# Opening of a hybrid decoder layer on one core: weight splits one piece ahead, squares of x in the order in which x lands, memory keys evacuated later, and another bank for a unit

## The chip, the cores and the metric

The kernel runs on one core of one Trainium2 chip. The metric is the device time of one execution in microseconds, the median of several runs. All times below are microseconds.

## What is computed

One decoder layer for 512 tokens of width 1024, in float32, with 256 memory tokens. Cut to what matters here:

```
h = rms_norm(x, g_mix)
proj = h @ w_in                       # queries, keys, values of two branches, q_c, three gates
mkv = rms_norm(mem, g_mem) @ w_mem_kv
mk, mv = split(mkv)                   # 512 columns of keys, 512 of values, 4 heads of 128
mk = rms_norm(heads(mk), g_k_mem);  q_c = rms_norm(heads(q_c), g_q_mem)
y_c = softmax(q_c mk^T / sqrt(128)) mv
merged = sigmoid(a_m) * (y_m @ w_br_moba) + sigmoid(a_f) * (y_f @ w_br_fox) + sigmoid(a_c) * (y_c @ w_br_mem)
x = x + merged @ w_out
x = x + (silu(h2 @ w_gate) * (h2 @ w_up)) @ w_down,   h2 = rms_norm(x, g_ffn)
```

y_m is block-sparse causal attention and y_f attention with a forgetting gate; neither is touched.

## The kernel before

**Products in three passes.** Each float32 operand is split into a high part, rounded to the fast float32 format of TensorE, and a low part, the rest. A product is hi·hi + hi·lo + lo·hi, three matmuls into one PSUM bank (PASSES). So each weight must be split before it is used.

**Pieces.** The weights come as a list of pieces, up to 512 KB each, laid out in the order of their use. `load_next` starts a piece's load on the queue of SP, into a tile `w_raw`. `split_next` issues ScalarE's copy to `w_hi` (L223) and puts VectorE's subtraction to `w_lo` (L226) off to the next call. `take` hands out the next piece; if it is not split yet, it is split then. Pieces 0 to 3 and 4 to 7 are the halves of `w_mem_kv` (keys and values of the memory), 8 to 11 the queries Q_C, and gates and units follow.

**The order of the work is fixed by the code, by ticks.** The engines run what they are given in program order. `mm` issues a matmul and, after every six matmuls of 512 columns, a `tick`. A tick splits one piece if fewer than `pace["ahead"]` pieces stand split beyond those taken, runs what `later(n, fn)` put off for n ticks, and then one step of the side list that `beside` filled. With `pace["ahead"] = 4`, set ahead of the keys, up to four pieces beyond the taken ones are split, and a split stands ahead of the tick's other steps.

**The opening.** `turn_mem` transposes the memory tokens and scales them into `mhT`. `mem_groups` (L497 to 513) makes two PSUM groups (two blocks of 128 memory tokens) over four pieces, first for the keys and then for the values: 48 matmuls of 512 columns each time. It takes both banks from the pool "m" (3 banks, `ps_m`); the pool "a" has 5 (`ps_a`). `head_chunk` (L515) evacuates the keys' groups at once (ScalarE's copy to `raw`, L523), squares them (`sqh`, L525) and sums the squares (VectorE, L526), and `head_rest` normalises them later. The values are evacuated to `memv` (ScalarE L318, VectorE L321). Beside these matmuls runs the side list: `square_x` (L622, ScalarE's sum of squares of one tile of 128 tokens of x), `rms_x` with `scale_x` (L627, tiles 0 and 1 on GpSimd, 2 and 3 on VectorE), `mem_square` (L455), `rms_mem`, and `turn_x` (L639), which transposes two of eight column blocks of x per step through a bank of "a" and evacuates them into `hT` (ScalarE's high part L318, VectorE's low part L321). When the values are done, the side list is flushed and `head_chunk` starts Q_C: its first group of 128 tokens takes the pieces 8 to 11, and `whole_h` (L652) adds up `xf` from `hT` on VectorE, one per tick.

**Units.** `tok_unit` makes 512 tokens by 512 columns from seven products M1 to M7 in the order M1, M2, M5, M6, M3, M7, M4, each in a bank of "m", but M5 in one of "a"; `after` adds each into its sums on VectorE one tick later (`add`, L745). It is called three times. What follows the second unit is `branch_part`, whose groups take banks of "m" and are evacuated by VectorE (L1047).

Of the kernel before, what the change touches and what calls it, by code (L numbers as in the profile page):

```python
# [13 lines left out]
AF = mybir.ActivationFunctionType  # L14
# [8 lines left out]
D = 1024  # L23
# [19 lines left out]
def hybrid_layer(ctx, tc, rope, x, mem, g_mix, w_in, b_forget, g_q_moba, g_k_moba, g_q_fox,  # L43
# [3 lines left out]
    act, dve, pool, pe = nc.scalar, nc.vector, nc.gpsimd, nc.tensor  # L47
# [8 lines left out]
    def slot(name, dt=F32):  # L56
        return U.tile([P, SLOT], dt, name=name, tag="u", bufs=NSLOT)
# [20 lines left out]
    def bank(tag):  # L78
        return psum.tile([P, 512], F32, name="ps_" + tag, tag=tag, bufs=BANKS[tag])

    def sm(name, w, bufs=6):
        return small.tile([P, w], F32, name=name, tag=name, bufs=bufs)
# [75 lines left out]
    raws, split, used = {}, {}, {}  # L158
# [82 lines left out]
    def take(n):  # L241
        while st["split"] < st["take"] + n:
            split_next(n)
        while w_lows:
            w_lows.popleft()()
        run_pend()
        got = [split.pop(st["take"] + j) for j in range(n)]
        st["take"] += n
        return got
# [6 lines left out]
    pace = {"credit": 0.0, "ns": 0, "ahead": 2}  # L256
    QUANTUM = 1250

    pend = []

    def run_pend():
        for fn in pend:
            fn()
        pend.clear()
# [42 lines left out]
    def later(n, fn):  # L307
        deferred.append([n, fn])
# [68 lines left out]
    def load_x():  # L377
        r = slot("x_t")
        t = len(x_t)
        nc.sync.dma_start(r[:, :D], x[0, t * P:(t + 1) * P, :])  # L380
        x_t.append(r)
# [11 lines left out]
    NG = 22  # L393
    GMIX, GFFN, GQF, GQM, GQC, GKF, GKM, GKC = 0, 8, 16, 17, 18, 19, 20, 21
    grow = consts.tile([NG, P], F32, name="grow")
    load_x()
    load_next()
    for _ in range(2):
        load_x()
    nc.gpsimd.dma_start(grow[0:8], g_mix.rearrange("o (k p) -> (o k) p", p=P))  # L400
    nc.gpsimd.dma_start(grow[8:16], g_ffn.rearrange("o (k p) -> (o k) p", p=P))
# [50 lines left out]
    ssp, ssm = sm("ssp", 4, 1), sm("ssm", 2, 1)  # L452
# [22 lines left out]

    def piece_of(W, k):
        for i in range(KD):
            if i == len(W):
                W.extend(take(1))
            n = W[i][0].shape[1]  # L480
            if k < n:
                return W[i], k
            k -= n

    def tok_group(lhs, t, W, n, tag="m"):


        ps = bank(tag)
        nk = len(lhs)
        for k in range(nk):  # L490
            w, j = piece_of(W, k)
            for a, b in PASSES:
                mm(ps[:, :n], lhs[k][a][:, t * P:(t + 1) * P], w[b][:, j, :n], n,
                   (k == 0 and (a, b) == PASSES[0]), (k == nk - 1 and (a, b) == PASSES[-1]))
        return ps

    def mem_groups(amid=None):  # L497


        ps = [bank("m"), bank("m")]  # L500
        for j in range(4):
            W = take(1)[0]
            todo = [(t, k, a, b) for t in range(MT) for k in (2 * j, 2 * j + 1) for a, b in PASSES]
            if amid and j == 0:
                todo.sort(key=lambda x: x[3])
            for n, (t, k, a, b) in enumerate(todo):
                if amid and j == 0 and n == 4:
                    amid()
                mm(ps[t], mhT[k][a][:, t * P:(t + 1) * P], W[b][:, k % 2, :], 512,
                   (k == 0 and (a, b) == PASSES[0]), (k == KD - 1 and (a, b) == PASSES[-1]))  # L510
        return ps

    def head_chunk(ntok, d, blocks, lag=9, pre=None, rows=None):


        W = []
        nh = 512 // d
        raws = [slot("raw") for _ in range(ntok // 2)]
        ss = sm("ss", 32, 4)
        for t in range(ntok):  # L520
            ps = tok_group(hT, t, W, 512) if pre is None else pre[t]
            r = raws[t // 2][:, t % 2 * 512:(t % 2 + 1) * 512]
            act.activation(r, ps, AF.Copy)  # L523
            sq = half_slot("sqh")
            act.activation(sq, r, AF.Square)  # L525
            pend.append(lambda t=t, sq=sq: dve.tensor_reduce(  # L526
                ss[:, t * nh:(t + 1) * nh], sq.rearrange("p (h d) -> p h d", h=nh),
                axis=AX.X, op=OP.add))
        head_rest(raws, 512, ss, ntok, d, "plain", blocks, lag, rows=rows)

    def head_rest(raws, tw, ss, ntok, d, kind, blocks, lag, rows=None, e=2):
# [85 lines left out]
    hT = []  # L617
# [3 lines left out]
    def square_x(t):  # L621
        act.activation(slot("junk")[:, :D], x_t[t][:, :D], AF.Square, accum_out=ssx[:, t:t + 1])  # L622
# [85 lines left out]
    def tok_unit(done):  # L708


        banks, raw = {}, {}
        z = half_slot("zs")

        def after(m):
            if m == "M1":
                act.activation(z, banks.pop(m), AF.Copy)
            elif m == "M2":
                raw[0] = slot("raw")
                add(raw[0][:, 0:512], banks.pop(m), z)
            elif m == "M6":  # L720
                add(z, banks.pop(m), z)
                add(raw[0][:, 512:1024], banks["M5"], z)
            elif m == "M3":
                add(raw[0][:, 512:1024], banks.pop(m), raw[0][:, 512:1024])
                done[0](raw[0])
            elif m == "M7":
                add(z, banks.pop(m), z)
                raw[1] = slot("raw")
                add(raw[1][:, 512:1024], banks.pop("M5"), z)
            elif m == "M4":  # L730
                add(raw[1][:, 0:512], banks.pop(m), z)
                done[1](raw[1])

        for m in ORDER:
            W = take(1)[0]
            ps = banks[m] = bank("a" if m == "M5" else "m")
            for t2 in range(2):
                for k in range(4):
                    for a, b in PASSES:
                        mm(ps[:, t2 * 256:(t2 + 1) * 256], right_of(RIGHT[m], k, a, t2), W[b][:, k, :],  # L740
                           256, (k == 0 and (a, b) == PASSES[0]), (k == 3 and (a, b) == PASSES[-1]))
            later(1, lambda m=m: after(m))
# [36 lines left out]
    rs_mem = sm("rsm", MT, 1)  # L779

    def rms_mem():
        dve.tensor_reduce(ssm, ssp.rearrange("p (t a) -> p t a", a=2), axis=AX.X, op=OP.add)
        rsqrt(ssm, 1.0 / D, 2, 1, out=rs_mem)

    def both(f, *args):
        return lambda: [f(*a) for a in args]

    def last_square(t):
        square_x(t)
        rms_x(t // 2)  # L790

    beside([idle, idle, small_gains, lambda: square_x(0), lambda: last_square(1),
            both(mem_square, (0, 0), (1, 0)), both(mem_square, (0, 1), (1, 1)),
            lambda: square_x(2), lambda: last_square(3), rms_mem, idle]
           + [both(turn_x, (k,), (k + 1,)) for k in range(0, KD, 2)], 1.0)

    turn_mem(0, (split_next, split_next))
    pace["ahead"] = 4
    pre = mem_groups(lambda: turn_mem(1))
    head_chunk(MT, 128, [(GKC, KC, h, gcol) for h in range(4)], lag=22, pre=pre, rows=rs_mem)  # L800
    vslots = [slot("memv", F32R) for _ in range(MT)]
    pre = mem_groups()
    for t in range(MT):
        evac_split(vslots[t][:, 0:512], vslots[t][:, 512:1024], pre[t], rs_mem[:, t:t + 1])
    pre = None
# [383 lines left out]
    B, L, H, banks, got, Z = {}, {}, {}, {}, {}, {}  # L1189
# [61 lines left out]
    for t in range(NT):  # L1251
        r = slot("x1")
# [392 lines left out]
    for n, x in enumerate(order):  # L1645
# [3 lines left out]
        _, m, p = x  # L1649
# [49 lines left out]
```

## Time and profile before

| what | us |
|---|---|
| median of 3 runs | 868.25 (867.46 to 868.31) |
| the profiled execution's own time | 868.44 |
| its span in the profile | 866.6 |
| TensorE's matmuls busy (PE) | 845.9, 98% |
| VectorE (DVE) | 659.1, 76% |
| ScalarE (ACT) | 471.9, 54% |
| GpSimd (POOL) | 226.2, 26% |

The page is one profiled execution. Busy time is the union of an engine's instructions; matmuls are pipelined, so that one row of several shows their common length, and one matmul alone shows its whole length. A number in square brackets behind a timeline row is the idle time of that engine just ahead of it and what ended it. The granted clock of TensorE is given as a share of full speed: 1.00 is 2.4 GHz and 0.50 is 1.2 GHz.

### The profile page before, as it was taken

How to read it: one execution, taken by the hardware profiler on the slowest of the kernel's cores; microseconds unless marked ns; L12 is line 12 of the kernel's file. 1: busy time of each engine (PE TensorE's matmuls, PEld its weight loads, DVE VectorE, ACT ScalarE, POOL GpSimd, SP SyncE). 2: the span in 40 equal slices, each digit the busy share in tenths (PEclk: the TensorE clock that was granted, in tenths of full speed). 3: DMA queues.
4: the chain of work that ended last, by engine and by line, in shares of the span. 5: the costliest groups of instructions: out<-in, count | busy, mean ns of one | idle time of the engine just before them, and what ended most of it. 6: DMA issues, size and time to landing. Idle time of an engine off the chain costs nothing.

```text
span 866.6 us, 13979 instructions
## 1 busy us (share of the span) xinstructions
PE 845.9 (98%) x5204; PEld 756.8 (87%) x5204; DVE 659.1 (76%) x1126; ACT 471.9 (54%) x816; POOL 226.2 (26%) x310
## 2 busy tenths in 40 slices
PE   7799999999999999999999999999999999999998
PEld 5588899799888888988888888999999999988886
DVE  5687599869678477667655936899889898997985
ACT  6755576567766546656534535454333444464671
POOL 5112228221522443434220003233210222110210
PEclk9899999999999999999999999999999999999999
DMA  9923248216430551441692535989885889774992
GB/s 311 339 34 88 59 115 213 39 50 193 114 86 11 162 142 29 135 106 52 179 211 97 171 97 122 216 182 191 169 173 92 177 164 205 178 188 147 232 257 94
DMA packets 141284, 126.10 MB, mean 146 GB/s; under 512 B 5841, under 2 KB 120073, under 8 KB 141217
## 3 DMA queue, kind: packets, MB, share of 16 engines
q1 hardware_dynamic: 107840, 95.21, 37.2%
q0 software_dynamic: 32192, 27.89, 21.0%
q10 hardware_dynamic: 1184, 2.12, 0.8%
q8 instruction: 41, 0.67, 0.3%
q14 instruction: 27, 0.21, 0.1%
HBM read 116.79 MB, written 4.21 MB: 140 GB/s over the span
## 4 chain that ended last, share of the span: by engine, by line
PE 80%; DVE 10%; ACT 5%; DMA 2%; issue 1%; POOL 1%; SPq 0%; DVEq 0%; ACTq 0%; POOLq 0%
PE ps_m L291 38%; PE ps_a L1369 12%; PE ps_m L1369 9%; PE ps_a L1522 9%; PE ps_a L959 3%; PE ps_m L1522 3%; DMA w_raw<-in_w_mem_kv_dram 2%; DVE w_lo L226 2%; PE ps_a L897 2%; PE ps_a L948 2%; ACT w_hi L223 1%; DVE wl L1230 1%; DVE w_sum L212 1%; DVE qT L587 1%; DVE xl L1315 1%
## 5 line engine op out<-in xcount | busy, mean ns | idle before, releaser
L226 DVE TENSOR_TENSOR w_lo<-w_raw,w_hi 128x1024 fp32r<-128x1024 f32 (+2 forms) x88 | 108.4, 1243 | 33.9 <-ACT w_hi L223 33.2
L291 PE MATMUL ps_m<-w_hi,hT 128*128 128x256 f32 (+2 forms) x464 | 122.0, 337 | 0.0
L291 PE MATMUL ps_m<-hT,w_hi 128*128 128x512 f32 x384 | 121.0, 396 | 0.0
L1369 PE MATMUL ps_a<-xh,wl 128*128 128x256 f32 x352 | 100.0, 284 | 1.0 <-DVE wl L1230 0.8
L1369 PE MATMUL ps_a<-xh,wh 128*128 128x256 f32 x352 | 99.8, 283 | 0.2 <-ACT wh L1227 0.2
L1369 PE MATMUL ps_a<-xl,wh 128*128 128x256 f32 x352 | 99.6, 283 | 0.0
L223 ACT ACTIVATE w_hi<-w_raw 128x1024 fp32r<-128x1024 f32 (+2 forms) x88 | 86.3, 1002 | 4.1 <-issue 2.5
L291 PEld LDWEIGHTS ps_m<-w_hi,hT 128*128 128x128 f32 x464 | 80.1, 189 | 7.1
L291 PEld LDWEIGHTS ps_m<-hT,w_hi 128*128 128x128 f32 x384 | 69.7, 189 | 12.8
L1522 PE MATMUL ps_a<-dh,dr 128*128 128x512 f32 x242 | 76.6, 390 | 0.1
L291 PE MATMUL ps_m<-w_lo,hT 128*128 128x256 f32 (+2 forms) x232 | 75.9, 327 | 0.0
L291 PE MATMUL ps_m<-hT,w_lo 128*128 128x512 f32 x192 | 75.0, 391 | 0.0
L1369 PE MATMUL ps_m<-xl,wh 128*128 128x256 f32 x264 | 74.7, 283 | 0.0
L1369 PE MATMUL ps_m<-xh,wh 128*128 128x256 f32 x264 | 74.7, 283 | 0.0
L1369 PE MATMUL ps_m<-xh,wl 128*128 128x256 f32 x264 | 74.7, 283 | 0.0
L1412 ACT ACTIVATE z<-z 128x512 f32<-128x512 f32 x22 | 13.9, 633 | 105.3 <-DVE z L745 105.3
L1204 POOL DMA_DIRECT2D wq<-in_w_gate_dram x22 | 30.6, 1389 | 153.2 <-DMA wq<-in_w_gate_dram 49.0
L1369 PEld LDWEIGHTS ps_a<-xh,wl 128*128 128x128 f32 x352 | 67.5, 192 | 1.6 <-DVE wl L1230 1.6
L1230 DVE TENSOR_TENSOR wl<-wq,wh 128x1024 fp32r<-128x1024 f32 x55 | 66.9, 1218 | 2.1 <-ACT wh L1227 1.6
L1369 PEld LDWEIGHTS ps_a<-xh,wh 128*128 128x128 f32 x352 | 67.5, 192 | 0.4 <-ACT wh L1227 0.4
L1369 PEld LDWEIGHTS ps_a<-xl,wh 128*128 128x128 f32 x352 | 67.6, 192 | 0.0
L930 POOL TENSOR_SCALAR p_t<-p_t,rc 128x128 f32<-128x128 f32 (+1 forms) x64 | 39.2, 613 | 108.1 <-DVE rc L929 92.9
(271 smaller groups left out, 2211.1 us busy)
## 6 DMA issues: line engine op xcount, KB each, us to landing
w_raw<-in_w_in_dram SPq DMA_DIRECT2D x45, 512.0 KB, 4.3
wq<-in_w_gate_dram SPq DMA_DIRECT2D x55, 256.0 KB, 5.2
wq<-in_w_up_dram SPq DMA_DIRECT2D x55, 256.0 KB, 5.7
dq<-in_w_down_dram SPq DMA_DIRECT2D x25, 512.0 KB, 5.9
wq<-in_w_gate_dram POOLq DMA_DIRECT2D x22, 256.0 KB, 7.9
wq<-in_w_up_dram POOLq DMA_DIRECT2D x22, 256.0 KB, 10.2
dq<-in_w_down_dram POOLq DMA_DIRECT2D x10, 512.0 KB, 8.2
w_raw<-in_w_mem_kv_dram SPq DMA_DIRECT2D x8, 512.0 KB, 8.9
```

The lines of the kernel that those rows point to most:

```text
L223: act.activation(hi[:, c], r[:, c], AF.Copy)
L226: dve.tensor_tensor(lo[:, c], r[:, c], f32(hi[:, c]), op=OP.subtract)
L291: pe.matmul(ps, lhsT, rhs, start=start, stop=stop)
L897: pe.matmul(ps[:, :n], Q[p][:, s * 512 + i * P:s * 512 + (i + 1) * P], K[p][s][:, b * 512:b * 512 + n], start=b == 0, stop=b == 1)
L930: pool.tensor_scalar(pt[:, :nk], pt[:, :nk], rc, 1.0, op0=OP.mult, op1=OP.mult)
L948: pe.transpose(tb[:, j * P:(j + 1) * P], pt[:, j * P:(j + 1) * P], ident)
L959: pe.matmul(yb[:, :256], V[p][:, j, 2 * s:2 * s + 2, :], PT[b][:, j, :], start=(j == 0 and b == 0), stop=(j == nj - 1 and b == 1))
L1204: e.dma_start(t[:, g * 512:(g + 1) * 512].rearrange("p (k c) -> p k c", k=4), dsrc(w, kh * 512 * DFF + f0 + fh * P, [[DFF, P], [P * DFF, 4 ...
L1230: dve.tensor_tensor(full(lo), full(r), f32(full(hi)), op=OP.subtract)
L1369: pe.matmul(ps[:, g * 256:(g + 1) * 256], w[a][:, g, k, :], r[b][:, k, :], start=n % 12 == 0, stop=n % 12 == 11)
L1412: act.activation(z[:, :, 0, :], z[:, :, 0, :], AF.Silu, scale=1.0 - 2 * j)
L1522: pe.matmul(acc_d[m][t2], r[a][:, e * 256 + t2 * P:e * 256 + (t2 + 1) * P], w[b][:, e * 512:(e + 1) * 512], start=(p == 0 and e == 0 and ( ...
```

## The change

Six edits, all on the order of things; every product and sum remains.

1. The loads: the fifth weight piece is loaded ahead of the second tile of x and not behind it.
2. `pace["ahead"]` stays 2 in the keys, becomes 1 with their last piece, and 4 with the last piece of the values (then 2, as before).
3. The side list squares the tiles 2 and 3 of x in one step, ahead of the second pair of memory squares; `rms_mem` runs after 12 ticks instead of in the list.
4. The evacuation of the keys is put off by 3 and 4 ticks, their squares by 5 and 6.
5. The second bank of the values comes from "a".
6. M4 of the units takes its bank from "a".

```diff
@@ -393,9 +393,8 @@
     NG = 22
     GMIX, GFFN, GQF, GQM, GQC, GKF, GKM, GKC = 0, 8, 16, 17, 18, 19, 20, 21
     grow = consts.tile([NG, P], F32, name="grow")
-    load_x()
     load_next()
-    for _ in range(2):
+    for _ in range(3):
         load_x()
     nc.gpsimd.dma_start(grow[0:8], g_mix.rearrange("o (k p) -> (o k) p", p=P))
     nc.gpsimd.dma_start(grow[8:16], g_ffn.rearrange("o (k p) -> (o k) p", p=P))
@@ -497,9 +496,11 @@
     def mem_groups(amid=None):
 
 
-        ps = [bank("m"), bank("m")]
+        ps = [bank("m"), bank("m" if amid else "a")]
         for j in range(4):
             W = take(1)[0]
+            if j == 3:
+                pace["ahead"] = 1 if amid else 4
             todo = [(t, k, a, b) for t in range(MT) for k in (2 * j, 2 * j + 1) for a, b in PASSES]
             if amid and j == 0:
                 todo.sort(key=lambda x: x[3])
@@ -517,15 +518,21 @@
         nh = 512 // d
         raws = [slot("raw") for _ in range(ntok // 2)]
         ss = sm("ss", 32, 4)
-        for t in range(ntok):
-            ps = tok_group(hT, t, W, 512) if pre is None else pre[t]
-            r = raws[t // 2][:, t % 2 * 512:(t % 2 + 1) * 512]
-            act.activation(r, ps, AF.Copy)
+        def square(t, r):
             sq = half_slot("sqh")
             act.activation(sq, r, AF.Square)
-            pend.append(lambda t=t, sq=sq: dve.tensor_reduce(
+            pend.append(lambda: dve.tensor_reduce(
                 ss[:, t * nh:(t + 1) * nh], sq.rearrange("p (h d) -> p h d", h=nh),
                 axis=AX.X, op=OP.add))
+
+        for t in range(ntok):
+            r = raws[t // 2][:, t % 2 * 512:(t % 2 + 1) * 512]
+            if pre is None:
+                act.activation(r, tok_group(hT, t, W, 512), AF.Copy)
+                square(t, r)
+            else:
+                later(3 + t, lambda r=r, ps=pre[t]: act.activation(r, ps, AF.Copy))
+                later(5 + t, lambda t=t, r=r: square(t, r))
         head_rest(raws, 512, ss, ntok, d, "plain", blocks, lag, rows=rows)
 
     def head_rest(raws, tw, ss, ntok, d, kind, blocks, lag, rows=None, e=2):
@@ -733,7 +740,7 @@
 
         for m in ORDER:
             W = take(1)[0]
-            ps = banks[m] = bank("a" if m == "M5" else "m")
+            ps = banks[m] = bank("a" if m in ("M5", "M4") else "m")
             for t2 in range(2):
                 for k in range(4):
                     for a, b in PASSES:
@@ -780,7 +787,7 @@
 
     def rms_mem():
         dve.tensor_reduce(ssm, ssp.rearrange("p (t a) -> p t a", a=2), axis=AX.X, op=OP.add)
-        rsqrt(ssm, 1.0 / D, 2, 1, out=rs_mem)
+        rsqrt(ssm, 1.0 / D, 2, 0, out=rs_mem)
 
     def both(f, *args):
         return lambda: [f(*a) for a in args]
@@ -790,12 +797,12 @@
         rms_x(t // 2)
 
     beside([idle, idle, small_gains, lambda: square_x(0), lambda: last_square(1),
-            both(mem_square, (0, 0), (1, 0)), both(mem_square, (0, 1), (1, 1)),
-            lambda: square_x(2), lambda: last_square(3), rms_mem, idle]
+            both(mem_square, (0, 0), (1, 0)), lambda: [square_x(2), last_square(3)], idle,
+            both(mem_square, (0, 1), (1, 1)), idle]
            + [both(turn_x, (k,), (k + 1,)) for k in range(0, KD, 2)], 1.0)
+    later(12, rms_mem)
 
     turn_mem(0, (split_next, split_next))
-    pace["ahead"] = 4
     pre = mem_groups(lambda: turn_mem(1))
     head_chunk(MT, 128, [(GKC, KC, h, gcol) for h in range(4)], lag=22, pre=pre, rows=rs_mem)
     vslots = [slot("memv", F32R) for _ in range(MT)]
```

On the queue of SP the first tiles of x (`x_t`) and the weight pieces (`w_raw`) stood so before:

```order
L380 DMA x_t_86<-in_x_dram 128x1024
L380 DMA x_t_94<-in_x_dram 128x1024
L179 DMA w_raw_96<-in_w_mem_kv_dram 128x2x512
L380 DMA x_t_98<-in_x_dram 128x1024
L380 DMA x_t_100<-in_x_dram 128x1024
```

and stand so now:

```order
L380 DMA x_t_86<-in_x_dram 128x1024
L179 DMA w_raw_94<-in_w_mem_kv_dram 128x2x512
L380 DMA x_t_96<-in_x_dram 128x1024
L380 DMA x_t_98<-in_x_dram 128x1024
L380 DMA x_t_100<-in_x_dram 128x1024
```

The piece has passed the second tile of x. ScalarE, from the split of the piece 5 on (`w_hi_284`, then 6, 7, 8), with the squares of the memory (`sqm`), the keys' evacuation and squares (`raw`, `sqh`) and the squares of x (`junk`), before:

```order
L223 ACTIVATE w_hi_284<-w_raw_200 128x1024
L455 ACTIVATE sqm_294,ssp_130<-mem_h_78 128x512 x2
L523 ACTIVATE raw_303<-ps_m_160 128x512
L525 ACTIVATE sqh_306<-raw_303 128x512
L523 ACTIVATE raw_303<-ps_m_161 128x512
L525 ACTIVATE sqh_306<-raw_303 128x512
L223 ACTIVATE w_hi_321<-w_raw_214 128x1024
L622 ACTIVATE junk_326,ssx_132<-x_t_98 128x1024
L223 ACTIVATE w_hi_335<-w_raw_252 128x1024
L622 ACTIVATE junk_340,ssx_132<-x_t_100 128x1024
L223 ACTIVATE w_hi_354<-w_raw_270 128x1024
```

and now, where the pieces 5, 6, 7 are `w_hi_314`, `w_hi_342` and `w_hi_378`:

```order
L629 ACTIVATE junk_289,ssx_132<-x_t_98 128x1024
L629 ACTIVATE junk_291,ssx_132<-x_t_100 128x1024
L223 ACTIVATE w_hi_314<-w_raw_200 128x1024
L347 ACTIVATE ra_295<-rv_293 128x2
L348 ACTIVATE ry_294<-ra_295 128x2
L454 ACTIVATE sqm_333,ssp_130<-mem_h_78 128x512 x2
L223 ACTIVATE w_hi_342<-w_raw_214 128x1024
L534 ACTIVATE raw_304<-ps_m_160 128x512
L534 ACTIVATE raw_304<-ps_m_161 128x512
L318 ACTIVATE hT_361<-ps_a_356,gcol_123 128x512
L318 ACTIVATE hT_369<-ps_a_364,gcol_123 128x512
```

The squares of x stand ahead of piece 5 and no longer behind 6 and 7; the keys' copies stand behind piece 6, their squares later still, and the first two evacuations of x ahead of piece 7.

VectorE around the start of Q_C, from the third low part of `hT` on; the pieces 8 to 10 had been split ahead of this, and `w_lo_450` is 11:

```order
L321 SCALAR_TENSOR_TENSOR hT_432<-ps_a_427,gcol_123,hT_432 128x512
L321 SCALAR_TENSOR_TENSOR hT_440<-ps_a_435,gcol_123,hT_440 128x512
L321 SCALAR_TENSOR_TENSOR hT_461<-ps_a_456,gcol_123,hT_461 128x512
L321 SCALAR_TENSOR_TENSOR hT_469<-ps_a_464,gcol_123,hT_469 128x512
L226 TENSOR_TENSOR w_lo_450<-w_raw_338,w_hi_449 128x1024
L321 SCALAR_TENSOR_TENSOR hT_484<-ps_a_479,gcol_123,hT_484 128x512
L321 SCALAR_TENSOR_TENSOR hT_492<-ps_a_487,gcol_123,hT_492 128x512
L321 SCALAR_TENSOR_TENSOR memv_314<-ps_m_316,rsm_133,memv_314 128x512
L321 SCALAR_TENSOR_TENSOR memv_315<-ps_m_317,rsm_133,memv_315 128x512
L652 TENSOR_TENSOR xf_509<-hT_406 128x512
L652 TENSOR_TENSOR xf_509<-hT_414 128x512
L652 TENSOR_TENSOR xf_529<-hT_432 128x512
```

and now from the seventh, where `w_lo_442`, `w_lo_473`, `w_lo_493` and `w_lo_510` are the pieces 8 to 11:

```order
L321 SCALAR_TENSOR_TENSOR hT_454<-ps_a_449,gcol_123,hT_454 128x512
L321 SCALAR_TENSOR_TENSOR hT_462<-ps_a_457,gcol_123,hT_462 128x512
L226 TENSOR_TENSOR w_lo_442<-w_raw_270,w_hi_441 128x1024
L321 SCALAR_TENSOR_TENSOR memv_310<-ps_m_312,rsm_133,memv_310 128x512
L321 SCALAR_TENSOR_TENSOR memv_311<-ps_a_313,rsm_133,memv_311 128x512
L226 TENSOR_TENSOR w_lo_473<-w_raw_317,w_hi_472 128x1024
L659 TENSOR_TENSOR xf_500<-hT_361 128x512
L226 TENSOR_TENSOR w_lo_493<-w_raw_345,w_hi_492 128x1024
L659 TENSOR_TENSOR xf_500<-hT_369 128x512
L226 TENSOR_TENSOR w_lo_510<-w_raw_381,w_hi_509 128x1024
```

The low parts of Q_C's four pieces stand now between the last evacuations and `xf`, one after the other. In the units, the sum of M4 reads `ps_a` instead of `ps_m`.

## Rows read from the trace of the kernel before

**Rows 1.** The page: the span, and the busy time of each engine (its share of the span, its instructions).

```profile
span 866.6 us, 13979 instructions
PE 845.9 (98%) x5204; PEld 756.8 (87%) x5204; DVE 659.1 (76%) x1126; ACT 471.9 (54%) x816; POOL 226.2 (26%) x310
```

**Rows 2.** The waits of TensorE, by what ended them: us in total, times, the longest.

```profile
PE ps_a L639 <- DVE x_t L627: 5.1, 2, 4.9
PE ps_m L291 <- DVE raw L745: 1.4, 1, 1.4
PE ps_m L291 <- ACT raw L523: 1.1, 1, 1.1
```

**Rows 3.** The chain of work that ended last, in order of time, from 36 to 62 us: start, length, engine and operation, count.

```profile
36.96 2.56 PE ps_m L291 x6
...
40.84 1.40 PE ps_m L291 x6
42.24 0.87 PE ps_a L639 x8
...
45.37 16.35 PE ps_m L291 x72
```

**Rows 4.** Windows: the stretch and its length, then the busy time (instructions) of PE, PEld, DVE, ACT and POOL, the granted clock of TensorE, the DMA share, GB/s.

```profile
33.50:40.30 6.80, 5.15 (x17) 4.17 (x18) 6.20 (x14) 2.59 (x5) 1.37 (x1) 0.50 1.08 340
...
22.73:52.03 29.30, 23.03 (x105) 18.62 (x104) 22.37 (x35) 21.15 (x35) 3.76 (x3) 0.88 0.92 261
...
60.00:70.00 10.00, 10.00 (x49) 8.18 (x48) 7.18 (x12) 5.50 (x9) 0.00 (x0) 1.00 0.00 0
...
80.00:90.00 10.00, 10.00 (x54) 8.45 (x53) 4.64 (x6) 5.05 (x7) 3.45 (x4) 1.00 0.73 159
```

**Rows 5.** The timeline of ScalarE in the opening: start, length, line, operation, tiles.

```profile
17.33 1.06 ACT L622 ACTIVATE junk<-x_t 128x1024 f32<-128x1024 f32 x1 [0.27 <-DMA x_t<-in_x_dram]
...
18.64 1.06 ACT L223 ACTIVATE w_hi<-w_raw 128x1024 fp32r<-128x1024 f32 x1 [0.16 <-DMA w_raw<-in_w_mem_kv_dram]
19.60 0.19 ACT L347 ACTIVATE ra<-rv 128x2 f32<-128x2 f32 x1
...
19.93 0.62 ACT L455 ACTIVATE sqm<-mem_h 128x512 f32<-128x512 f32 x1
...
22.58 1.06 ACT L223 ACTIVATE w_hi<-w_raw 128x1024 fp32r<-128x1024 f32 x1 [1.32 <-DMA w_raw<-in_w_mem_kv_dram]
...
24.77 0.57 ACT L523 ACTIVATE raw<-ps_m 128x512 f32<-128x512 f32 x1
25.37 0.63 ACT L525 ACTIVATE sqh<-raw 128x512 f32<-128x512 f32 x1
...
28.01 1.05 ACT L622 ACTIVATE junk<-x_t 128x1024 f32<-128x1024 f32 x1
...
42.72 1.27 ACT L318 ACTIVATE hT<-ps_a,gcol 128x512 fp32r<-128x512 f32 x2
...
52.23 0.60 ACT L523 ACTIVATE raw<-ps_m 128x512 f32<-128x512 f32 x1 [2.86 <-PE ps_m L291]
```

**Rows 6.** The timeline of TensorE's matmuls: the values' first matmul in its second bank, and the last matmul of Q_C's first group (the first of the two).

```profile
25.39 0.50 PE L291 MATMUL ps_m<-w_hi,mhT 128*128 128x512 f32 x1 [1.15 <-ACT raw L523]
...
51.81 0.62 PE L291 MATMUL ps_m<-w_hi,hT 128*128 128x512 f32 x2
```

**Rows 7.** The timeline of VectorE in the opening.

```profile
26.04 0.69 DVE L526 TENSOR_REDUCE ss<-sqh 128x4 f32<-128x512 f32 x1 [1.14 <-ACT sqh L525]
...
32.44 1.22 DVE L226 TENSOR_TENSOR w_lo<-w_raw,w_hi 128x1024 fp32r<-128x1024 f32 x1
33.58 0.16 DVE L351 TENSOR_TENSOR ra<-ry 128x2 f32<-128x2 f32 x1
...
34.16 1.42 DVE L627 TENSOR_SCALAR x_t<-x_t,rr 128x1024 f32<-128x1024 f32 x2
...
47.22 1.40 DVE L321 SCALAR_TENSOR_TENSOR memv<-ps_m,rsm,memv 128x512 fp32r<-128x512 f32 x2
48.53 1.88 DVE L652 TENSOR_TENSOR xf<-hT 128x512 f32<-128x512 f32 x3
```

**Rows 8.** The timeline of TensorE and VectorE behind the second unit: matmuls of `branch_part`, the sum of M4 (L745) and the first group's evacuation (L1047).

```profile
156.70 0.39 PE L291 MATMUL ps_m<-yT,w_lo 128*128 128x512 f32 x1
...
157.61 0.69 DVE L745 TENSOR_TENSOR raw<-ps_m,zs 128x512 f32<-128x512 f32 x1
...
158.45 0.70 PE L291 MATMUL ps_m<-yT,w_hi 128*128 128x512 f32 x2 [1.36 <-DVE raw L745]
...
159.13 0.68 DVE L1047 SCALAR_TENSOR_TENSOR acc<-th,ps_m 128x512 f32<-128x512 f32 x1
```

**Rows 9.** The timeline of GpSimd and VectorE at two places: the opening, and a stretch near 300 us in which GpSimd computes.

```profile
38.39 1.22 DVE L226 TENSOR_TENSOR w_lo<-w_raw,w_hi 128x1024 fp32r<-128x1024 f32 x1
38.66 1.37 POOL L184 DMA_DIRECT2D w_raw<-in_w_in_dram  x1 [14.83 <-DMA w_raw<-in_w_in_dram]
...
298.06 7.03 POOL L1148 TENSOR_TENSOR ckb<-ckb,mz 128x512 f32<-128x512 f32 x4
299.30 4.63 DVE L226 TENSOR_TENSOR w_lo<-w_raw,w_hi 128x1024 fp32r<-128x1024 f32 x2 [5.35 <-ACT w_hi L223]
```

## The prediction

> **What bounds the kernel now.** I read the page first, then TensorE's waits, the chain of waits, windows, and the timelines of the opening. The page [rows 1] shows TensorE's matmuls busy for 845.9 of 866.6 us. So only time in which TensorE idles or runs at half clock can be won, and the edits touch two such places. TensorE's waits [rows 2] name them: 5.1 us for scaled tiles of x and 1.1 for the keys' evacuation, both in the opening, and 1.4 for the sum of M4.
>
> The opening is the stretch from 22.73 (first matmul of piece 4) to 52.03 (end of Q_C's first group), 29.30 us [rows 4]. Its work at full speed: 48 matmuls of the values and 24 of Q_C's first group at 16.35/72 = 0.227 each, and 32 transposes at 0.87/8 = 0.109 [rows 3], 16.34 + 3.49 = 19.83. So 9.5 us are lost. The wait behind the keys' evacuation is 1.15 [rows 6], those for x 5.1 [rows 2], and from 33.5 to 40.3 the granted clock was 0.50 [rows 4], the 1.2 GHz level: it fell in the idle stretch of 4.9. Six matmuls then took 2.56 against 1.40 [rows 3], so the 5.15 us that were busy at that level held 5.15 × (1 − 1.40/2.56) = 2.3 too much. These make 8.6; the rest is idle time of under a microsecond around the waits.
>
> Why x is late is seen on ScalarE and VectorE [rows 5, 7]. ScalarE squares tile 2 at 28.01, behind four operations on the keys and the splits of pieces 5 and 6. After the last square VectorE has two low parts (the one at 32.44 is the second) and the root's three small steps to do before it scales at 34.16.
>
> **Edits 1 to 4 together: x ready earlier.** Lengths are from one start to the next, since an engine begins the next operation some 0.09 before a row's own end: a high part 0.96 (18.64 to 19.60, where its row says 1.06) and the root's two steps 0.33 (19.60 to 19.93). With the same overlap a square of x takes 1.04 with the reading of its sum, a pair of memory squares 1.23, a copy of the keys 0.49 (0.57), their square 0.54 (0.63), a pair of evacuations 1.18 (1.27), all [rows 5].
>
> Piece 4 now lands at about 17.33, where tile 1 did, and tile 1 at 18.64, where piece 4 did. I take this exchange whole: both are 512 KB on one queue. ScalarE: square of tile 1 until 19.68, piece 4's high part 20.64, root 20.97, memory squares 22.20, squares of tiles 2 and 3 until 24.28. Piece 5 has landed at 22.58, so the load is not what is waited for; its high part ends at 25.34 against 23.54 before. That is dearer: VectorE's low part then ends at 26.60 (1.22) where TensorE, without its wait for a bank (edit 5), ends piece 4 at 25.45. A new wait of about 1.0 takes the place of the 1.15 removed. VectorE does the root by 27.10 (0.58, from 33.58 to 34.16 [rows 7]) and scales both tiles by 28.52 (1.42), against 35.6 before. The transposes that need tile 3 then wait some 0.45 us instead of 4.9. GpSimd scales tile 1 about 1 us later than before, still ahead of 28.5.
>
> **What is late next: VectorE.** The splits taken out of the keys come back behind x. ScalarE goes on: root 25.57, memory squares 26.80, piece 6 27.76, keys' copies 28.74, two evacuations of x 29.92, piece 7 30.88, a key square 31.42, the next evacuation 32.11. From there VectorE has no gap to the end of Q_C's first group. In its order of issue stand four pairs of 1.32 (three of `hT`, one of `memv`; 47.22 to 48.53), five low parts for pieces 7 to 11 (1.13 each, 32.44 to 33.58 less 0.01; the last with its whole 1.22), two sums of 0.60 (0.69 less the overlap), the root's 0.58, a tiny step 0.09 and two `xf` of 0.60 (0.68 less the overlap, by the three in 1.88), all [rows 7]. Sum: 5.28 + 5.74 + 1.20 + 0.58 + 0.09 + 1.20 = 14.09, so VectorE ends piece 11's low part at 46.23. TensorE has five matmuls left after that; the last one starts 0.93 later at 47.17. In before the last started at 51.81 [rows 6] and ScalarE's copy of the group at 52.23 [rows 5], so this copy comes at 47.59. **That is 4.6 us earlier.** For gaps of 0.03 between engines at some of the crossings I take off 0.2: −4.4.
>
> The other way round: TensorE then waits 1.0 and 0.45 in the values and some 3.5 in Q_C's group (1.6 for piece 8's low part, which stands behind the evacuations, then 1.1, 0.4, 0.4). That is 5.0 lost instead of 9.5, the same sum. The half clock goes too, if no idle stretch is long enough to lose it; the longest now is the 1.6.
>
> Bounds for the opening: if VectorE's operations don't overlap at all (16 of them, 0.085 each), 1.4 is lost: −3.2. If tile 1 still lands at 17.33, all on ScalarE is up to 1.3 earlier: −5.9.
>
> **Edit 5, alone,** removes the 1.15 of the bank; it is priced above, since the low part of piece 5 takes the place of nearly all of it. The bank from "a" costs nothing as long as `turn_x` finds its banks free, and it needs two at a time out of five.
>
> **Edit 6: M4's bank.** The wait of 1.36 behind the second unit [rows 2, 8] is the third group of `branch_part`, which needs M4's bank until VectorE has read it (157.61 + 0.69). With M4 in "a" that group's bank was free long before, so it starts at 157.09. It lasts 12 × 0.227 = 2.72, until 159.81 by start; the fourth group then needs the bank of the first, read at 159.13 + 0.68 = 159.81. So a wait of some 0.2 or none is left: I take −1.2, with bounds of 0 and −1.36.
>
> **Sum:** 868.44 − 4.4 − 1.2 = **862.8**. The profiled execution's own time, 868.44, lies 0.19 above the median of the runs; the span 866.6 is 1.8 less, which I take as unchanged.
>
> **Rivals.** A difference of 0.2% (1.7 us) is what a measurement of this kernel can tell from none; so faster is below 866.5 and slower above 870.0.
>
> *The clock falls again.* The 1.6 us of waiting for piece 8 stands beside idle stretches of 1.15 and 1.36 after which the clock stayed, and of 4.9 in which it fell. It is nearer to the former. If it falls, about the 2.3 to 2.4 of before are paid again: 865.2.
>
> *M4's bank gives nothing:* the fourth group waits for what the third did, or VectorE's sums of the second unit come later anyway. 864.0.
>
> *TensorE's lead is given back.* VectorE sets the pace past 52 us up to the next waits of about 1 us near 107, and the 4.4 come to nothing; M4's bank is left: 867.2. For it: VectorE is behind TensorE in Q_C's group in the changed order. Against: it is busy for only 7.18 of 10 us from 60 to 70, and 4.64 from 80 to 90, with TensorE busy for 10.00 in both [rows 4]; so it catches up.
>
> *VectorE's operations don't overlap.* Then its chain is 1.4 longer, the opening gives 3.2 and the time is 864.0. Against: the low part at 32.44 lasts 1.22, and the next operation begins 1.14 after it [rows 7]. [...]
>
> *GpSimd blocks VectorE (slower).* In the stretch near 300 two low parts took 4.63, 2.3 each, beside GpSimd's additions [rows 9]. If the five low parts of the chain from 32.11 met such work, the cost is 5 × 1.1 = 5.5; TensorE's wait for piece 8 then grows from 1.6 to 3.8 (two low parts ahead of it), and the clock falls for 2.4 more: 862.8 + 5.5 + 2.4 = 870.7. It becomes slower from about 0.95 per low part on. For it: these low parts now decide TensorE's start, which they did not before. Against: GpSimd has only two issues of a DMA in this stretch, and the one at 38.66 stood beside a low part of 1.22, no longer than any other [rows 9].
>
> The Trainium skill, SBUF — State Buffer, section SBUF: two separate sides, says that a VectorE operation with two SBUF inputs and a GpSimd operation that reads SBUF share a port pair as an exclusive lock, the other blocking fully. The rows near 300 agree; the row at 38.39 shows that the issues of a DMA don't do it.
>
> **How the numbers follow.** Forecast 862.8: 0.72, its own range by the bounds 861.2 (−5.9 − 1.36) to 864.0 (−3.2 − 1.2). Clock falls 0.08 (865.2), M4 gives nothing 0.07 (864.0), no overlap 0.03 (864.0), lead given back 0.06 (867.2), blocked 0.04 (870.7). The range 861.2 to 865.4 takes in the first four. Faster 0.90, the same 0.06, slower 0.04.
>
> **What would show it.** Right: ScalarE squares tile 3 before 24.5; VectorE scales it by 28.6; the granted clock is 1.00 from 33 to 40; four new waits of TensorE for `w_lo` in Q_C's first group, 3 to 4 us in all; ScalarE's copy of that group at 47 to 48 and not 52.23; no wait for L745's successor near 153 us. Wrong: an idle stretch of over 2 us with a clock of 0.50 behind it, a wait at 107 that shrinks, or low parts of over 1.3 us.

## The result

The changed kernel takes 862.68 us (862.43 to 863.07, 4 runs), the kernel before beside it 868.28: a ratio of 0.9938 (0.9920 to 0.9955). The forecast was 862.8. The profiled execution took 862.71.

The page of the changed kernel, the lines that answer to [rows 1], and its row of TensorE's granted clock, in tenths of full speed by slices of 21.5 us (rounded down, so that 9 is 0.9 or more):

```profile
span 860.9 us, 13979 instructions
...
PE 844.2 (98%) x5204; PEld 754.4 (88%) x5204; DVE 658.6 (77%) x1126; ACT 470.8 (55%) x816; POOL 225.8 (26%) x310
...
PEclk9999999999999999999999999999999999999999
```

The same row of the kernel before:

```profile
PEclk9899999999999999999999999999999999999999
```

The span is 5.7 us shorter, and the slice with an 8 in the clock's row is gone. TensorE's waits, where [rows 2] had 4.9 for a tile of x, 1.4 for M4's sum and 1.1 for the keys:

```profile
PE ps_m L291 <- DVE w_lo L226: 3.0, 4, 1.3
```

All three are gone. In their place stand waits for low parts of weights: of the four in this row one of 0.22 is in the keys, one of 0.76 in the values, and two, of 1.28 and 0.79, in Q_C's first group. The windows that answer to [rows 4] (the same columns), up to ScalarE's copy of Q_C's first group:

```profile
33.50:40.30 6.80, 6.00 (x34) 4.81 (x32) 6.73 (x13) 6.32 (x12) 1.37 (x1) 1.00 1.10 344
40.30:48.18 7.88, 6.45 (x24) 4.38 (x25) 7.88 (x10) 3.50 (x4) 1.29 (x1) 1.00 0.87 145
```

The clock is at 1.00 where it was 0.50. VectorE is busy for 7.88 of the last 7.88 us, TensorE for 6.45: TensorE's waits there are for low parts that VectorE makes, so VectorE sets the end. ScalarE's timeline, against [rows 5]:

```profile
19.07 1.06 ACT L629 ACTIVATE junk<-x_t 128x1024 f32<-128x1024 f32 x1 [1.97 <-DMA x_t<-in_x_dram]
...
20.13 1.04 ACT L223 ACTIVATE w_hi<-w_raw 128x1024 fp32r<-128x1024 f32 x1
...
23.67 1.05 ACT L629 ACTIVATE junk<-x_t 128x1024 f32<-128x1024 f32 x1
...
24.71 1.04 ACT L223 ACTIVATE w_hi<-w_raw 128x1024 fp32r<-128x1024 f32 x1
...
48.18 0.60 ACT L531 ACTIVATE raw<-ps_m 128x512 f32<-128x512 f32 x1 [4.38 <-PE ps_m L291]
```

The last square of x started at 30.00 in the kernel before:

```profile
30.00 1.04 ACT L622 ACTIVATE junk<-x_t 128x1024 f32<-128x1024 f32 x1
```

Now it starts at 23.67, and Q_C's first group is copied at 48.18 instead of 52.23. The first row above matters for what follows: ScalarE waits 1.97 us for tile 1 of x, which in the kernel before cost 0.27.

VectorE and TensorE, against [rows 6 to 8]:

```profile
27.51 1.42 DVE L634 TENSOR_SCALAR x_t<-x_t,rr 128x1024 f32<-128x1024 f32 x2
...
32.69 1.41 DVE L321 SCALAR_TENSOR_TENSOR hT<-ps_a,gcol,hT 128x512 fp32r<-128x512 f32 x2 [1.15 <-ACT hT L318]
...
45.43 1.22 DVE L226 TENSOR_TENSOR w_lo<-w_raw,w_hi 128x1024 fp32r<-128x1024 f32 x1
```

```profile
39.11 0.39 PE L291 MATMUL ps_m<-w_hi,hT 128*128 128x512 f32 x1
40.77 0.50 PE L291 MATMUL ps_m<-w_lo,hT 128*128 128x512 f32 x1 [1.28 <-DVE w_lo L226]
...
43.22 0.50 PE L291 MATMUL ps_m<-w_lo,hT 128*128 128x512 f32 x1 [0.79 <-DVE w_lo L226]
...
152.67 0.39 PE L291 MATMUL ps_m<-yT,w_lo 128*128 128x512 f32 x1
152.89 0.61 PE L291 MATMUL ps_m<-yT,w_hi 128*128 128x512 f32 x2
```

The scaling ends at 28.93 instead of 35.58. From 32.69 VectorE runs without a gap of more than 0.04 to the end of piece 11's low part, 46.65. The matmul of 152.89 is the one that waited 1.36 at 158.45 before. It now follows its neighbour by 0.22.

**Where the time came from.** Matmul by matmul, TensorE is 4.03 us earlier from the second group of Q_C on (53.17 before, 49.14 now), 5.56 earlier at that matmul of `branch_part`, 5.64 at the next one, and 5.7 at the end. So the opening gave 4.0 us and M4's bank 1.6: 1.53 for the wait, and 0.08 because the matmul behind a wait is followed by the next after 0.31 us and not after 0.23. The rest of the program gave less than 0.1.

### The profile page after: what moved, and what is told of

Read it like the earlier page. It is cut to its first block, busy times and chain, and to the rows that moved or that the text cites. A ratio compares the mean times of both kernels' runs of the same rounds, so it can differ in the third digit from the quotient of the medians.

```text
span 860.9 us, 13979 instructions
## 1 busy us (share of the span) xinstructions
PE 844.2 (98%) x5204; PEld 754.4 (88%) x5204; DVE 658.6 (77%) x1126; ACT 470.8 (55%) x816; POOL 225.8 (26%) x310
## 3 DMA queue, kind: packets, MB, share of 16 engines
q10 hardware_dynamic: 1184, 2.12, 0.8%
## 4 chain that ended last, share of the span: by engine, by line
PE 82%; DVE 9%; ACT 5%; DMA 2%; issue 1%; SPq 0%; ACTq 0%; DVEq 0%
PE ps_m L291 39%; PE ps_a L1376 12%; PE ps_m L1376 9%; PE ps_a L1529 9%; PE ps_a L966 3%; PE ps_m L1529 3%; PE ps_a L904 2%; PE ps_a L955 2%; PE ps_a L291 2%; DMA x_t<-in_x_dram 2%; DVE w_lo L226 2%; DVE wl L1237 1%; ACT w_hi L223 1%; PE ps_a L578 1%; DVE xl L1322 1%
## 5 line engine op out<-in xcount | busy, mean ns | idle before, releaser
L1211 POOL DMA_DIRECT2D wq<-in_w_gate_dram x22 | 32.5, 1478 | 153.0 <-DMA wq<-in_w_gate_dram 67.5
```

Of the source, the lines that this page charges most:

```text
L1211: e.dma_start(t[:, g * 512:(g + 1) * 512].rearrange("p (k c) -> p k c", k=4), dsrc(w, kh * 512 * DFF + f0 + fh * P, [[DFF, P], [P * DFF, 4 ...
```

## The experiments

The theory: ScalarE and VectorE bring x too late in the kernel before; the order of the squares of x mends that; after it VectorE's chain of low parts sets the end of Q_C's first group; M4's bank is a term by itself. The rival that I took most seriously: the splitting one piece ahead, which the change is named after, is what brings x forward. Ratios are to the kernel before, run on the same chip beside it. It took 868.07 beside the first four experiments, 867.71 beside the change again, the two edits and the last one, and 867.90 beside the others; so a difference between times of two groups is uncertain by some 0.4.

**M4's bank undone** (the changed kernel otherwise).

```diff
-            ps = banks[m] = bank("a" if m in ("M5", "M4") else "m")
+            ps = banks[m] = bank("a" if m == "M5" else "m")
```

> The changed kernel (862.68) with M4's bank from "m" again. Theory: the wait behind the second unit returns at its place near 153 us. Its first matmul started 1.55 us earlier with edit 6 than the matmuls ahead of it did (4.01 us earlier before it, 5.56 behind it), so 864.2, and the opening stays as it is. Rival: VectorE's and ScalarE's rows there stayed at 4.0 us earlier for another 18 us, so they may set the pace and the wait may be paid anyway: 862.7.

864.56 (863.52 to 865.88), ratio to before 0.9960 (0.9947 to 0.9972). Its waits hold the old row again:

```profile
PE ps_m L291 <- DVE raw L752: 1.4, 1, 1.4
```

Against the profile of the changed kernel its matmuls are 1.63 us late at 53 us and 3.13 late at the matmul behind this wait: the bank is worth 1.50 there, as expected, and 1.58 from the next matmul on. The 1.63 are not M4's: ScalarE got tile 1 of x at 20.74 in this execution, not at 19.07.

**The order of loads undone.**

```diff
-    load_next()
-    for _ in range(3):
-        load_x()
+    load_x()
+    load_next()
+    for _ in range(2):
+        load_x()
```

> The changed kernel with the old order of the first loads (tile 1 of x ahead of piece 4). Theory: edit 1 costs time. In the changed kernel ScalarE stood idle for 1.97 us until tile 1 came at 19.07; with the old order its square starts at about 17.33 and piece 4's high part at 18.64 instead of 20.13, 1.5 us earlier, and all of ScalarE's and then VectorE's chain follows, so Q_C's first group ends about 1.4 us earlier: 861.3 (861.0 to 862.0). Rival: the order of the loads is part of the gain, since piece 4 is needed first: 862.7 or slower, up to 864.2.

861.69 (860.96 to 861.76), ratio 0.9923 (0.9910 to 0.9937). ScalarE in this kernel:

```profile
17.93 1.06 ACT L630 ACTIVATE junk<-x_t 128x1024 f32<-128x1024 f32 x1 [0.70 <-DMA x_t<-in_x_dram]
...
19.23 1.06 ACT L223 ACTIVATE w_hi<-w_raw 128x1024 fp32r<-128x1024 f32 x1 [0.15 <-DMA w_raw<-in_w_mem_kv_dram]
```

So edit 1 costs about 1 us: no run of this kernel was as slow as any of the nine of the changed kernel (862.43 to 863.39), though the intervals of the ratios overlap, and at 53 us its matmuls stand 0.93 ahead of the changed kernel's. ScalarE's program has tile 1's square ahead of piece 4's high part. In the changed kernel piece 4 landed at 17.80, and its high part began at 20.13: the engine idled for the tile while the piece that it could have worked on stood behind it in its program.

**Four pieces split ahead, as before** (edit 2 undone).

```diff
-            if j == 3:
-                pace["ahead"] = 1 if amid else 4
...
+    pace["ahead"] = 4
     pre = mem_groups(lambda: turn_mem(1))
```

> The changed kernel with four pieces split ahead from the start of the keys, as before (edit 2 undone), the rest kept. Theory A: it is the order of the squares of x (edit 3) that brings x forward. The scaling of tiles 2 and 3 then stands behind one more low part (1.13) and comes 0.9 to 1.2 us later, the piece 4 wait grows, but the low parts of pieces 8 to 10 are done ahead of Q_C, so that the waits of 3.0 us there go: 1 us or so faster than the change, 861.6 (861 to 862.5). Theory B: it is the splitting one ahead that brings x forward; without it the scaling comes near 35 us again, TensorE idles for over 4 us and the clock falls: 866 to 868.

862.38 (861.54 to 863.74), ratio 0.9937 (0.9924 to 0.9949): not to be told from the change. The profiled execution, of 863.74:

```profile
28.43 0.50 PE L291 MATMUL ps_m<-w_lo,mhT 128*128 128x512 f32 x1 [2.02 <-DVE w_lo L226]
30.82 0.48 PE L644 MATMUL ps_a<-ident,x_t 128*128 128x128 f32 x1 [0.33 <-DVE x_t L632]
```

```profile
29.50:36.00 6.50, 5.99 (x20) 4.41 (x19) 6.12 (x11) 6.47 (x12) 0.00 (x0) 0.50 1.08 349
```

Theory B falls: x is not late without edit 2 (a wait of 0.33, not 4.9). None of Q_C's waits is left either, as theory A has it. But a wait of 2.02 in the values has come, the clock fell behind it, and ScalarE got tile 1 at 19.98 in this execution. VectorE shows where the wait is from:

```profile
27.08 0.17 DVE L343 TENSOR_SCALAR rv<-ssx 128x2 f32<-128x2 f32 x1 [3.28 <-ACT junk L627]
27.16 2.35 DVE L226 TENSOR_TENSOR w_lo<-w_raw,w_hi 128x1024 fp32r<-128x1024 f32 x2
```

It idled 3.28 us for the squares of x, whose root stands ahead of piece 5's low part in its program. The two runs with the mean clock at 0.996 took 863.5 and 863.7, the one at 0.998 took 861.7, and the two at 1.000 took 861.5 and 862.4.

**The squares' order undone** (edit 3, without the move of `rms_mem`).

```diff
-            both(mem_square, (0, 0), (1, 0)), lambda: [square_x(2), last_square(3)], idle,
-            both(mem_square, (0, 1), (1, 1)), idle]
+            both(mem_square, (0, 0), (1, 0)), both(mem_square, (0, 1), (1, 1)),
+            lambda: square_x(2), lambda: last_square(3), idle, idle]
```

> The changed kernel with the side list's old order of squares (both pairs of memory squares ahead of the squares of tiles 2 and 3, these in two steps). Theory A (the order of the squares): ScalarE's squares stand behind another pair of memory squares and the high part of piece 5, the scaling comes about 1.5 us later; TensorE waits 1.5 us for x instead of 0.45, and a part is won back since VectorE's chain is then the same: 863.2 to 864.2. Theory B (the splits): no difference, 862.7.

864.62 (864.27 to 865.52), ratio 0.9962 (0.9949 to 0.9974): theory B's 862.7 is out, and it is more than A expected. Of the 1.80 us that it lost by 53 us in the profile, tile 1's later landing (20.04) may explain up to 0.97, the squares the rest. TensorE waited 1.05 for x here, and 2.12 for a low part in Q_C's first group:

```profile
31.47 0.33 PE L646 MATMUL ps_a<-ident,x_t 128*128 128x128 f32 x1 [1.05 <-DVE x_t L634]
...
45.07 0.50 PE L291 MATMUL ps_m<-w_lo,hT 128*128 128x512 f32 x1 [2.12 <-DVE w_lo L226]
```

So x comes earlier by the other edits too: without the new order of squares the wait for x is 1.05 and not 4.9, and the kernel is still 3.45 us faster than before. Which of them does it was not run alone; ScalarE squares tile 2 at 25.78 here and not at 28.01, no longer behind four operations on the keys and piece 6's high part.

**The squares' order alone,** on the kernel before.

```diff
-            both(mem_square, (0, 0), (1, 0)), both(mem_square, (0, 1), (1, 1)),
-            lambda: square_x(2), lambda: last_square(3), rms_mem, idle]
+            both(mem_square, (0, 0), (1, 0)), lambda: [square_x(2), last_square(3)], idle,
+            both(mem_square, (0, 1), (1, 1)), rms_mem, idle]
```

> The kernel before with one edit: tiles 2 and 3 of x squared in one step ahead of the second pair of memory squares (the memory's root stays in the list, two steps later). Theory A, the order of the squares carries most of the opening's gain: ScalarE squares tile 3 before 26 instead of at 31, VectorE scales both tiles by about 32 instead of 35.6, TensorE's wait for x falls from 4.9 to 1 to 1.5, and the low parts of pieces 8 to 10 are still done ahead of Q_C, so none of the waits for them comes. The keys' evacuation is now 2.1 us later, so the wait for its bank grows from 1.15 to 2 to 3. Together 3 to 4.5 less than before without M4's: 863.5 to 865 (2 more where the clock falls in the bank's wait). Theory B, all of edits 1 to 5 are needed: 867.0 or more.

863.97 (863.60 to 864.14), ratio 0.9956 (0.9942 to 0.9969): one edit of two lines gives 3.9 us of the 5.6 (`rms_mem` keeps its place in the list). Its waits:

```profile
PE ps_m L291 <- ACT raw L523: 2.3, 1, 2.3
...
PE ps_m L291 <- DVE raw L745: 1.4, 1, 1.4
```

```profile
26.77 0.50 PE L291 MATMUL ps_m<-w_hi,mhT 128*128 128x512 f32 x1 [2.34 <-ACT raw L523]
```

The wait for x is not among them any more; the bank's wait has grown from 1.15 to 2.34, since the keys' copies stand behind two squares of x, and M4's is as before. No wait for a low part is left in Q_C's first group. Its matmuls are 4.9 us ahead of the kernel before at 53 us, more than the 4.0 of the whole change, and 4.2 from 67 us on, for a transposition of the keys now waits 0.41 for GpSimd at 57.38.

**Two edits: the squares' order and M4's bank,** on the kernel before (the diff just above, and edit 6).

> The kernel before with two of the six edits: tiles 2 and 3 of x squared ahead of the second pair of memory squares, and M4's bank from "a". Theory: the first alone gave 863.97 and the second is worth 1.5 at its own place, so 862.5, the time of all six edits. Rival: the two don't add, since VectorE lies closer behind TensorE near 150 us: 863.3 or more.

862.04 (861.36 to 862.65), ratio 0.9931 (0.9919 to 0.9944). Two of the six edits give what all six give. Of the other four one costs a microsecond; with that one left out (861.69 above) the remaining three are ahead of the two edits by 0.35 us, with ranges of runs that overlap. So these four are worth little on top of the two, though they bring a part of the gain where the squares' order is missing.

**The change again,** without any edit, beside the two edits:

> The changed kernel once more, on this chip and beside the two below. Theory, that the old order of loads is the better one: the time scatters upward from 862.4, as the second tile of x landed between 19.1 and 20.7 us in the four profiles with this order of loads (17.3 to 17.9 in the old order), so 862.4 to 864.0, median 862.7 to 863.5. Rival: it stays at 862.4 to 863.1, and the scatter was another chip's.

862.95 (862.73 to 863.39), ratio 0.9943 (0.9929 to 0.9956); tile 1 was squared from 19.22. The median fits both; the scatter was small here, 0.66 us, as the rival has it. In the five profiles with the new order of loads this square starts at 19.07, 19.22, 19.98, 20.04 and 20.74; in the kernels with the old order that were profiled, at 17.01 to 17.93.

**The keys evacuated at once,** with the old order of loads.

```diff
-                later(3 + t, lambda r=r, ps=pre[t]: act.activation(r, ps, AF.Copy))
-                later(5 + t, lambda t=t, r=r: square(t, r))
+                act.activation(r, pre[t], AF.Copy)
+                square(t, r)
```

> The changed kernel with the old order of the first loads (861.7) and with the keys evacuated and squared at once on ScalarE (edit 4 undone as well). Theory: four operations, 2.1 us, stand ahead of piece 5's high part; TensorE has about 1 us of slack there, so it waits 1.5 to 2 for that high part and then 1 for the low part, x comes 2 us later, and VectorE's chain about 1 us later, since two sums of squares (1.2) are then done ahead of it: 862.7 (862 to 863.2; 2 more where the clock falls). Rival: with the bank from "a" nobody waits for the keys, and putting them off is worth nothing: 861.7.

862.36 (861.99 to 864.31), ratio 0.9945 (0.9932 to 0.9957). Its profile has the waits that were expected, smaller: 0.96 for piece 5's high part and 0.76 for its low part. The rival is not excluded by the times, for the ratio overlaps that of the same kernel with the keys put off (0.9910 to 0.9937). At 53 us its matmuls are 0.65 behind that kernel's, although tile 1 was squared 0.5 earlier in it (17.42 against 17.93). So putting the keys off is worth some 0.6 to 1.2 us here by two profiles, and is not shown by the times.

**The second bank from "m",** with the old order of loads.

```diff
-        ps = [bank("m"), bank("m" if amid else "a")]
+        ps = [bank("m"), bank("m")]
```

> The changed kernel with the old order of the first loads (861.7) and with the second bank of the values from "m" again (edit 5 undone as well). Theory: edit 4 needs edit 5. The values' second group then waits for the copy of the keys' first group, which now stands behind piece 6's high part: TensorE idles from about 23.6 to 27.3, 3.7 us; the time is 2.5 to 3 longer, and more than 2 us of idle lets the clock fall, for 1 to 2.4 more: 864.5 to 867. Rival: the bank is hidden and the wait of 1.15 in before was all that it could cost: 861.7 to 862.8.

865.69 (863.83 to 866.33, 10 runs), ratio 0.9971 (0.9962 to 0.9980).

```profile
27.87 0.50 PE L291 MATMUL ps_m<-w_hi,mhT 128*128 128x512 f32 x1 [3.62 <-ACT raw L535]
```

```profile
28.00:30.00 2.00, 2.00 (x8) 1.62 (x9) 1.14 (x2) 0.30 (x1) 0.00 (x0) 0.83 1.08 369
30.00:32.00 2.00, 2.00 (x7) 1.42 (x6) 0.00 (x0) 0.00 (x0) 0.00 (x0) 0.50 1.12 356
```

As expected: beside edit 4 the bank from "m" costs 4.0 us, so edit 4 needs edit 5. (Edit 4 alone, on the kernel before, was not run.) The clock fell behind the 3.6 us of idle time in this execution. Two of the ten runs kept a mean clock of 1.000 and took 863.8 and 863.9; the eight at 0.998 took 865.2 to 866.3, about 2 us more.

**VectorE's chain made shorter,** with the old order of loads.

```diff
-                later(5 + t, lambda t=t, r=r: square(t, r))
+                later(13 + t, lambda t=t, r=r: square(t, r))
...
-    sums_of_h(1)
+    sums_of_h(6)
```

> The changed kernel with the old order of the first loads (861.7), and with four operations taken out of VectorE's chain into Q_C's later groups: the two sums of the keys' squares (0.60 each, with ScalarE's squares) 8 ticks later, and the sums of h (xf, 0.60 each) five ticks later. Nothing is left out. Theory: VectorE's chain sets the end of Q_C's first group, and TensorE's waits there (1.28, 0.78 and two of about 0.2 to 0.4) shrink by what is taken out: 2.0 to 2.3 faster, 859.5. Rival: TensorE's waits there are paid back behind it or the moved work is late further on (the keys' normalisation, the sums of h for the units): 861.7 or more.

859.42 (859.15 to 859.69), ratio 0.9905 (0.9891 to 0.9918). One wait for a low part is left in Q_C, of 0.78. Four operations of 0.60 us, moved behind Q_C's first group, gave 2.3 us, as they should if VectorE's chain sets the end of that group. Not all of it need be theirs: of the 2.48 that this kernel's matmuls are ahead of the kernel with the long chain at 53 us, 0.55 stood already at 28.9, ahead of Q_C, since ScalarE got tile 1 at 17.37 and not at 17.93; and ScalarE's two squares of the keys moved along, so that its evacuations of x came earlier too. Some 0.3 us was paid back later (2.18 ahead at 256 us).

**And the splits let ahead step by step,** on top of that.

```diff
             if j == 3:
                 pace["ahead"] = 1 if amid else 4
+            if j == 1 and not amid:
+                pace["ahead"] = 2
+            if j == 2 and not amid:
+                pace["ahead"] = 3
```

> The kernel with the shorter chain (859.42), and the splits let ahead step by step in the values: one piece ahead until the second piece is taken, then two, then three, then four. Theory: one wait of 0.78 for piece 9's low part was left in Q_C; low parts move from Q_C into the stretch in which VectorE still had idle time (30 to 38 us, busy 6.9 of 8 in the last), and the wait shrinks: 858.7 (858.5 to 859.2). Rival: the low parts then stand ahead of the evacuations of x and make these late: 859.4 to 860.5.

858.36 (857.97 to 858.82), ratio 0.9889 (0.9875 to 0.9902): faster than both kernels, 4.6 us below the changed one beside it. The wait in Q_C is down to 0.24, and VectorE is busy for 7.93 of the 8 us from 30 to 38 and for all of the next 8:

```profile
42.37 0.50 PE L291 MATMUL ps_m<-w_lo,hT 128*128 128x512 f32 x1 [0.24 <-DVE w_lo L226]
```

```profile
30.00:38.00 8.00, 8.00 (x48) 6.86 (x46) 7.93 (x16) 7.53 (x13) 0.00 (x0) 1.00 1.09 346
38.00:46.00 8.00, 7.76 (x35) 6.10 (x34) 8.00 (x11) 5.32 (x9) 2.66 (x2) 1.00 0.82 184
```

## Why the prediction was right

**x earlier, VectorE late next.** Right in place, and nearly in size. The scaling ended at 28.93 (forecast 28.52), and VectorE's chain took 13.96 us (32.69 to 46.65, forecast 14.09). That this chain binds is seen in the trace, in which VectorE has no gap and TensorE waits for its low parts, and the run that shortens it agrees. VectorE's operations did overlap: the rows of the chain add up to 15.4, since most begin 0.08 to 0.09 before the row ahead of them ends. The Trainium skill, VectorE: DVE Perf Modes, section The DRAIN you can't avoid, says that an operation that is not held back starts before the pipe of the one ahead of it is empty; the trace agrees.

**The opening's sum** was 4.0 us and not 4.4. The term that was mis-sized is the exchange of tile 1 and piece 4 that I "took whole": the step from the first to the second was as taken (1.27 us; 1.31 before), but piece 4, now the first, landed at 17.80 and not at about 17.33, so that tile 1 came at 19.07 and not 18.64 and everything on ScalarE 0.43 later. My bound for the case in which the tile still came at 17.33 was the useful number: with the old order of loads the opening gave 4.95, with the tile at 17.93. I priced that case and did not see that it is the better kernel. Two signs were missed narrowly, mostly by this: the scaling by 28.6 (28.93) and the copy of Q_C's first group at 47 to 48 (48.18). The end of piece 11's low part at 46.23 was also 0.03 off in the adding up; 32.11 and 14.09 make 46.20.

**The waits.** In the values the forecast wait of 1.0 came as 0.24 for piece 5's high part and 0.76 for its low part; of the 0.45 for the tiles of x no wait above 0.15 shows. In Q_C I forecast 1.6, 1.1, 0.4 and 0.4, together 3.5; by the starts of matmuls, less 0.227, they are 1.44, 0.96, 0.25 and 0.25, together 2.9, and the matmul behind each is followed 0.11 late, which makes 3.3. The trace's waits show only 1.28 and 0.79 of these, because the modelled end of a matmul (0.39) reaches over the next one's turn.

**M4's bank** gave 1.6 (1.50 to 1.58 in the run that undid it), and not 1.2; it lies outside my bound of 1.36. That bound was the trace's idle time, which starts at a modelled end: by starts the wait was 158.45 − 156.70 − 0.227 = 1.52. And the fourth group does not wait at all. The two misses, 0.4 too much and 0.4 too little, cancel: that the total came within 0.2 us is luck, and the parts are good to 0.4.

**The clock** stayed at 1.00 with waits up to 1.28, as forecast. **The lead** of 4.0 us did not melt: TensorE's matmuls keep it from 53 us up to M4's wait. **GpSimd** did not block VectorE: the five low parts of the chain took 1.21 to 1.22. The row at 38.39 that I leaned on began ahead of GpSimd's issue; better evidence is that 21 low parts of the changed kernel that began within such an issue, and met no computing of GpSimd, took 1.21 to 1.23.

**What the prediction did not say** is which edit does it. "Edits 1 to 4 together" hid that the order of the squares alone gives nearly all of the opening, that without it the other edits still bring much of it, that the order of loads costs a microsecond, and that the keys put off need the bank from "a". It also hid what the splitting one ahead trades: without it a wait of 2.02 opens in the values and the waits in Q_C go, and the time is the same.

## What to carry to other kernels

Where one late product holds everything (here the scaled tiles of x), move its own chain ahead on each engine first, and measure that edit alone: it may be nearly the whole gain. Then leave it out of the full change as well: here the two answers differ (3.9 us alone, 1.9 at most lost when undone). Load in the order in which the engine's program consumes; here a piece loaded earlier cost time, since ScalarE's program had another tile ahead of it. When work is pushed out of one bound stretch, count what the same engine must do in the next one; there the low parts came back, and moving what nobody waits for yet, with the splits in smaller steps, was worth another 3.3 us (861.69 to 858.36), of which up to 0.6 may be tile 1's earlier landing (17.35 and not 17.93 in the profiles).

## What the runs showed of the hardware

The granted clock fell to 0.50 behind idle stretches of TensorE of 2.02, 2.34 and 3.62 us and within one of 4.93, and stayed at 1.00 behind 1.15, 1.28, 1.36, 1.37 and also 2.12 us. The last is the wait that ended at 45.07 in the kernel with the squares' order undone (the columns of [rows 4], with the clock seventh):

```profile
45.00:52.00 7.00, 6.78 (x27) 4.98 (x28) 7.00 (x10) 1.79 (x3) 1.29 (x1) 1.00 0.64 91
```

So the length of the idle stretch alone does not decide, and "more than 2 us", as an expectation above has it, does not hold. What goes with a fall differs. With 3.62 us of idle time the runs that lost the clock took about 2 us longer. In the profile of one of them it is at 0.50 for 3.4 us (29.3 to 32.7), of which the half clock can have taken half, 1.7, at most; what else differed between these runs is open, as only one was profiled. With 2.34 the runs at a mean clock of 0.998 (863.9 to 864.1) and of 1.000 (863.6 to 864.0) hardly differ.

With piece 4 loaded ahead of tile 1 of x, both 512 KB on one queue, ScalarE's square of the tile began 1.26 to 1.27 us behind the piece's landing in all five profiles. What varies is that landing: 17.8, 18.0, 18.7, 18.8 and 19.5 us, where the tile in the piece's place landed at 16.8 to 17.9 in the eight profiles with the old order. Why the piece comes later, and varies more, was not tried.
